# Selection masks, candidate pairs and expert tiles in the routing of a gMLP, attention and PEER block

## The chip, the cores and the metric

One core of a Trainium2 chip runs the whole program. The metric is the device time of one execution in microseconds (us). The engines are TensorE (PE, with its weight loads as PEld), VectorE (DVE), ScalarE (ACT), GpSimd (POOL) and the DMA queues that SyncE (SP), ACT and POOL issue. Each engine runs its own instructions in order; semaphores tie the engines together.

## The reference

For 512 tokens of width 1024 the block adds a mixing branch and then an expert branch. What the change touches is the expert branch (PEER): eight heads each score 2 x 128 sub keys, keep the best 16 of either half, form the sums of pairs, keep the best 16 pairs, and so choose 16 of 16,384 experts.

```python
q = (xb @ w_query).reshape(PEER_TOKEN_BLOCK, PEER_HEADS, 2, PEER_HALF)
sc = jnp.einsum('thpd,hpkd->thpk', q, sub_keys).astype(jnp.float32)
s_top, i_top = lax.top_k(sc, PEER_TOPK)
cand = s_top[:, :, 0, :, None] + s_top[:, :, 1, None, :]
cand_idx = i_top[:, :, 0, :, None] * PEER_NKEYS + i_top[:, :, 1, None, :]
...
best, pos = lax.top_k(cand, PEER_TOPK)
eidx = jnp.take_along_axis(cand_idx, pos, axis=-1)
g = jax.nn.softmax(best, axis=-1)
u = jnp.take(expert_u, eidx, axis=0)
h = jax.nn.gelu(jnp.einsum('thkd,td->thk', u, xb))
vv = jnp.take(expert_v, eidx, axis=0)
return jnp.einsum('thk,thkd->td', (g * h.astype(jnp.float32)).astype(xb.dtype), vv)
```

## The kernel before

The 512 tokens are four tiles of 128. The program runs in four stages: mixing (to about 240 us), routing (to about 455 us), gates (to about 622 us) and the loop over expert chunks (to the end).

**Dense and gathered tokens.** Three token tiles (ND = 3), less their last 64 tokens, do the expert branch densely: 128 expert tiles, each a load of 512 KB (`raw`), a split into `hi` (ACT, line 124) and `lo` (line 125, on DVE or POOL), and 24 matmuls of 320 columns (three products for each of 8 depth steps, lines 140 to 142) into one of two PSUM buffers `pu`, which ACT empties with a GELU into `act` (line 546). Sums of such tiles are later multiplied with gates and with the rows of `expert_v`. The remaining 64 tokens have their rows of `expert_u` gathered: 64 "early rows" of 128 x 1024, each an indirect DMA on POOL (line 480) and a dot product on DVE (line 489, one operand `xbu` in PSUM). The first token tile is gathered wholly in the last stage.

**Routing.** Iteration h of the loop in lines 665 to 684 issues up to EARLY = 7 early rows into ROWA = 8 row buffers, then `candidates(h)`: two projections of 24 matmuls of 512 columns each into PSUM tiles `pa` (four buffers), one expert tile before the key scores and one after (FILL = 1, counted in chunks of two tiles), eight small key-score products (line 649), and the top 16 of six score tiles on DVE (`top16`, 30 instructions). Then `pairs` and `choose` of the head before: `pairs` copies positions to floats on ACT (lines 580, 581) and adds pairs on DVE, seven `tensor_tensor` instructions with both operands in SBUF (line 588). `choose` spreads the pair indices into `tree` (line 595, a copy on POOL), takes the top 16 of the pair sums, makes six bit masks of the positions in one `tensor_tensor` of the positions and a constant `bits` (line 601, both in SBUF, result in a PSUM tile `pa`), and selects with them in six predicated copies (line 613). The result `eidx` (line 615) feeds the row indices of the next early rows (line 495). After head 7 an iteration without a head makes BRIDGE = 8 expert tiles, the softmax over all heads follows (line 621), and routing ends. By then 26 expert tiles are begun (2 + 16 + 8).

**Gates.** Lines 779 to 831 are written out in order for PE, DVE, ACT and POOL. `indices_of` turns `eidx` into two index rows (lines 703 to 706), `gates_of` transposes them on PE (lines 712 to 714). Then 48 steps, each of 8 tokens: DVE makes two one-hot arrays `bm` and `am` (lines 728, 738), POOL multiplies `bm` by the gates (line 730), ACT makes a part of `am` (lines 742, 744), PE multiplies them (line 751, 16 instructions a step) and ACT copies the result out (line 754); every two steps 1 MB is stored. Beside that a step issues one early row while there are any, and multiplies a few depth steps of an expert tile so that 40 tiles are done after the last step (`made`, `left`, `some`); six more follow.

**Order.** In routing a scheduler orders each engine's instructions by priority and its own estimates. In the gate stage the order is the code's. In the loop PE's order is the code's. A PSUM or SBUF tile of a pool with n buffers waits until the tile n allocations earlier has been read for the last time: the mask tile of head h takes a `pa` buffer that the second key-score tile of head h + 2 takes after it.

```python
nc.vector.tensor_tensor(mask.rearrange("p (l n) -> p l n", l=6),
                        bpos.rearrange("p t k -> p (t k)")[:, None, :]
                        .to_broadcast([P, 6, n * TOPK]),
                        bits[:, :, None].to_broadcast([P, 6, n * TOPK]), op=ALU.bitwise_and)
```

## Time and profile before

| what | value |
| --- | --- |
| median of three runs | 1493.92 us (1490.16 to 1494.91) |
| the profiled execution's own time | 1489.67 us |
| its span, first to last instruction | 1487.9 us |
| mean granted TensorE clock | 0.984 of full speed |
| PE busy, share of the span | 94% |
| DVE | 78% |
| ACT | 43% |
| POOL | 46% |

Shares of the whole span hide the stages, so the rows below go stage by stage: first the busy time of each engine in each stretch, then single instructions. Idle time in a row stands in brackets with what ended it. In the table of stretches a PE that is busy for the whole stretch is the bound there; a PE with idle time while DVE is busy for the whole stretch is not.

### The profile page before, as it was taken

What the parts mean: (1) busy time and instruction counts of PE and PEld (TensorE: products, weight loads), DVE (VectorE), ACT (ScalarE), POOL (GpSimd) and SP (SyncE); (2) the same over time, 40 slices, a digit from 0 to 9 for tenths busy, and PEclk for the clock granted to TensorE, in tenths of its full rate; (3) what the DMA queues carried; (4) which work ended last, traced back from release to release, by engine and by line L of the source; (5) the groups of instructions that cost most, each with busy time, mean ns of one, the idle gap of its engine ahead of it and who ended that gap; (6) DMA issues with size and microseconds to landing.
All of it is one profiled execution on the core that took longest, in us unless ns stands there. A gap on an engine that the chain in (4) does not pass through costs nothing.

```text
span 1487.9 us, 21702 instructions
## 1 busy us (share of the span) xinstructions
PE 1403.9 (94%) x7804; PEld 1235.9 (83%) x7804; DVE 1158.7 (78%) x2345; ACT 641.9 (43%) x1108; POOL 690.4 (46%) x470
## 2 busy tenths in 40 slices
PE   7999999998878888999989899999999999999998
PEld 6886678987777888888978799888999989888886
DVE  5437554699996968688988789898888888688883
ACT  5447534332335677743434333343343333333331
POOL 0000016687867966504435555464555554344530
PEclk9999999998998999999999999999999999999999
DMA  5352226576765976878878799999999999879992
GB/s 184 114 184 71 86 102 186 184 260 230 282 230 165 324 219 198 240 256 310 300 284 331 290 376 330 350 355 349 389 350 357 368 341 367 305 285 341 333 356 85
DMA packets 161420, 396.78 MB, mean 267 GB/s; under 512 B 12304, under 2 KB 74528, under 8 KB 159264
## 3 DMA queue, kind: packets, MB, share of 16 engines
q1 hardware_dynamic: 62992, 197.42, 37.4%
q0 software_dynamic: 47488, 171.50, 31.1%
q10 hardware_dynamic: 50832, 26.48, 6.3%
q8 instruction: 61, 1.00, 0.3%
q14 instruction: 47, 0.39, 0.1%
HBM read 363.86 MB, written 31.46 MB: 266 GB/s over the span
## 4 chain that ended last, share of the span: by engine, by line
PE 51%; DVE 19%; DMA 13%; issue 7%; POOL 5%; ACT 4%; ACTq 0%; SPq 0%; DVEq 0%; POOLq 0%
PE pu L140 6%; PE pu L142 6%; PE pu L141 6%; PE pa L932 5%; PE pa L933 5%; PE pa L936 5%; DMA row<-in_vd,eint 5%; DVE rowe L489 3%; PE px L933 3%; PE px L932 3%; PE px L936 3%; DMA row<-in_ud,eint 3%; PE pa L140 2%; PE pa L141 2%; PE pa L142 2%
## 5 line engine op out<-in xcount | busy, mean ns | idle before, releaser
L124 ACT ACTIVATE hi<-raw 128x1024 fp32r<-128x1024 f32 x300 | 317.3, 1058 | 511.0 <-DMA raw<-in_vd 185.2
L125 DVE TENSOR_TENSOR lo<-raw,hi 128x1024 fp32r<-128x1024 f32 x251 | 309.5, 1234 | 109.5 <-ACT hi L124 108.4
L874 POOL DMA_INDIRECT row<-in_vd,eint x128 | 196.9, 1538 | 196.8 <-DVE acc L876 165.2
L863 POOL DMA_INDIRECT row<-in_ud,eint x128 | 184.6, 1442 | 190.3 <-DVE row L865 149.1
L140 PE MATMUL pu<-xch,hi 128*128 128x320 f32 x816 | 257.7, 316 | 3.5 <-ACT act L546 2.9
L142 PE MATMUL pu<-xch,lo 128*128 128x320 f32 x816 | 252.6, 310 | 2.6 <-POOL lo L125 2.0
L141 PE MATMUL pu<-xcl,hi 128*128 128x320 f32 x816 | 252.5, 309 | 0.0
L932 PE MATMUL pa<-hi,wh 128*128 128x512 f32 x512 | 200.9, 392 | 0.0
L933 PE MATMUL pa<-lo,wh 128*128 128x512 f32 x512 | 200.5, 392 | 0.0
L876 DVE SCALAR_TENSOR_TENSOR acc<-row,hw,acc 128x1024 f32<-128x1024 f32 x128 | 165.1, 1290 | 40.4 <-DMA row<-in_vd,eint 40.1
L865 DVE SCALAR_TENSOR_TENSOR row<-row,xb 128x1024 f32<-128x1024 f32 x128 | 156.3, 1223 | 28.9 <-DMA row<-in_ud,eint 28.5
L140 PEld LDWEIGHTS pu<-xch,hi 128*128 128x128 f32 x816 | 154.7, 190 | 7.2 <-ACT act L546 5.0
L936 PE MATMUL pa<-hi,wl 128*128 128x512 f32 x512 | 158.1, 390 | 0.0
L142 PEld LDWEIGHTS pu<-xch,lo 128*128 128x128 f32 x816 | 154.3, 189 | 3.8 <-POOL lo L125 2.2
L141 PEld LDWEIGHTS pu<-xcl,hi 128*128 128x128 f32 x816 | 154.6, 189 | 1.5
L125 POOL TENSOR_TENSOR lo<-raw,hi 128x1024 fp32r<-128x1024 f32 x49 | 117.8, 2416 | 77.2 <-ACT hi L124 73.3
L751 PE MATMUL pa<-bm,am 128*128 128x128 f32 x768 | 99.0, 283 | 19.9 <-POOL bm L730 13.7
L751 PEld LDWEIGHTS pa<-bm,am 128*128 128x128 f32 x768 | 93.3, 196 | 25.1 <-POOL bm L730 22.6
L932 PEld LDWEIGHTS pa<-hi,wh 128*128 128x128 f32 x512 | 96.8, 189 | 20.6
L933 PEld LDWEIGHTS pa<-lo,wh 128*128 128x128 f32 x512 | 96.8, 189 | 20.5
L936 PEld LDWEIGHTS pa<-hi,wl 128*128 128x128 f32 x512 | 96.6, 189 | 20.6
L933 PE MATMUL px<-lo,wh 128*128 128x512 f32 x256 | 101.0, 395 | 7.2 <-DVE lo L125 7.2
(215 smaller groups left out, 2635.1 us busy)
## 6 DMA issues: line engine op xcount, KB each, us to landing
raw<-in_uT SPq DMA_DIRECT2D x128, 512.0 KB, 5.8
raw<-in_vd SPq DMA_DIRECT2D x128, 512.0 KB, 5.6
gd<-gst ACTq DMA_DIRECT2D x24, 1024.0 KB, 6.2
gc<-gd SPq DMA_DIRECT2D x15, 1536.0 KB, 9.7
raw<-in_w_in SPq DMA_DIRECT2D x20, 512.0 KB, 4.7
raw<-in_wq SPq DMA_DIRECT2D x16, 512.0 KB, 3.8
raw<-in_w_out SPq DMA_DIRECT2D x8, 512.0 KB, 4.2
bt<-in_bias SPq DMA_DIRECT2D x8, 256.0 KB, 7.4
```

The costliest lines, as they stand in the source:

```text
L124: nc.scalar.activation(hi, raw, AF.Copy)
L125: eng.tensor_tensor(lo, raw, hi.bitcast(F32), op=ALU.subtract)
L140: nc.tensor.matmul(ps, lh[0], rh[0], start=first, stop=False)
L141: nc.tensor.matmul(ps, lh[0], rh[1], start=False, stop=False)
L142: nc.tensor.matmul(ps, lh[1], rh[0], start=False, stop=last)
L751: nc.tensor.matmul(ps[:, i * P:(i + 1) * P], am[:, 4 * q + i, :], bm[:, 4 * q + i, :], start=True, stop=True)
L863: nc.gpsimd.indirect_dma_start(out=row, out_offset=None, in_=ud, in_offset=bass.IndirectOffsetOnAxis(ap=eint[:, j:j + 1], axis=0))
L874: nc.gpsimd.indirect_dma_start(out=row, out_offset=None, in_=vd, in_offset=bass.IndirectOffsetOnAxis(ap=eint[:, j:j + 1], axis=0))
L876: nc.vector.scalar_tensor_tensor(acc0, row, hw[:, j:j + 1], acc0, op0=ALU.mult, op1=ALU.add)
L932: nc.tensor.matmul(accs[t][half], wh[:, b, tok], w[b][0][:, ds_], start=first, stop=False)
L933: nc.tensor.matmul(accs[t][half], wh[:, b, tok], w[b][1][:, ds_], start=False, stop=False)
L936: nc.tensor.matmul(accs[t][half], wl[:, b, tok], w[b][0][:, ds_], start=False, stop=last)
```

## The change

In routing, six `tensor_scalar` instructions, one for each bit, take the place of the one mask instruction and its constant `bits`. `pairs` gets a part of the mask's PSUM tile, into which ACT copies the best scores and the scaled positions of the first half; the seven additions read them there and their other operand in SBUF. The tree copy goes from POOL to ACT. Six early rows instead of seven are issued for each head, into six buffers instead of eight. FILL becomes a list in tiles: two for heads 0 to 3, three for heads 4 to 7, so that 30 tiles are begun in routing instead of 26; `act` slots are taken when a tile is opened. `pairs` of the last head and the softmax are not scheduled before the fourth and the sixth of the eight bridging tiles has been activated. `indices_of` of the first gate tile and the split of two more expert tiles go ahead of the softmax's end, and the gate stage begins with one whole expert tile before and another after its first transposes. In the gate stage the last tile's `gates_of` is made two steps earlier. In the last stage `choose` uses the six instructions too, with masks in SBUF and the tree copy on POOL as before.

```diff
-ROWA = 8
+ROWA = 6
-EARLY = 7
+EARLY = 6
-SOME = 14
-FILL = 1
+SOME = 15
+FILL = (2, 2, 2, 2, 3, 3, 3, 3)
...
-        def pairs(pool, top, pos, n):
-
-            nc.scalar.activation(top[:, 1, :, 0, :], pos[:, :, 0, :], AF.Copy, scale=float(NK))
+        def pairs(pool, top, pos, n, ps=None):
+
+            if ps is None:
+                first = top[:, :, :, 0, :]
+            else:
+                first = ps.rearrange("p (a t r) -> p a t r", a=2, r=TOPK)
+                nc.scalar.copy(first[:, 0], top[:, 0, :, 0, :])
+            nc.scalar.activation(first[:, 1], pos[:, :, 0, :], AF.Copy, scale=float(NK))
...
-                                        a[:, :, 0, i:j, None].to_broadcast(full), op=ALU.add)
+                                        f[:, :, i:j, None].to_broadcast(full), op=ALU.add)
...
-            nc.gpsimd.tensor_copy(tree, cand[:, 1, :, None, 0:32].to_broadcast([P, n, TOPK, 32]))
+            spread(tree, cand[:, 1, :, None, 0:32].to_broadcast([P, n, TOPK, 32]))
...
-            nc.vector.tensor_tensor(mask.rearrange("p (l n) -> p l n", l=6),
-                                    bpos.rearrange("p t k -> p (t k)")[:, None, :]
-                                    .to_broadcast([P, 6, n * TOPK]),
-                                    bits[:, :, None].to_broadcast([P, 6, n * TOPK]), op=ALU.bitwise_and)
+            for i in range(6):
+                nc.vector.tensor_scalar(mask[:, i * n * TOPK:(i + 1) * n * TOPK], bpos.rearrange("p t k -> p (t k)"),
+                                        1 << i, None, op0=ALU.bitwise_and)
...
-                for _ in first_products(len(acts) * BC, BRIDGE, nc.gpsimd, True):
-                    pass
+                for i, _ in enumerate(first_products(sum(FILL) + BC, BRIDGE, nc.gpsimd, True)):
+                    behind.append(done[0])
...
-                mask = pa()[:, 0:6 * ND * TOPK].bitcast(U32)
+                ps = pa()
+                mask = ps[:, 0:6 * ND * TOPK].bitcast(U32)
...
-                choose(rq, pairs(rq, *cands.pop(0), ND), ND, gate[:, GT:, hs], eidx[:, GT:, hs], mask, tree)
+                with tc.issue_after(behind[BRIDGE // 2 - 1]) if behind else ExitStack():
+                    cand = pairs(rq, *cands.pop(0), ND, ps[:, 6 * ND * TOPK:8 * ND * TOPK])
+                choose(rq, cand, ND, gate[:, GT:, hs], eidx[:, GT:, hs], mask, tree, nc.scalar.copy)
...
-        softmax(rq, gate[:, GT:, :].rearrange("p t (h k) -> p (t h) k", k=TOPK), ND * NH)
+        ff = {0: indices_of(GT)}
...
+        for _ in range(HELD):
+            split_next()
+        with tc.issue_after(behind[-3]):
+            softmax(rq, gate[:, GT:, :].rearrange("p t (h k) -> p (t h) k", k=TOPK), ND * NH)
...
-            ff[0] = indices_of(GT)
-            split_next()
+            multiply_tile()
             gs[0] = gates_of(GT, ff.pop(0))
             split_next()
+            multiply_tile()
```

On DVE in routing, head 0, this stood from the mask on before (`pa` is the mask, `top`, `pos` and `scr` belong to the keys of a later head):

```order
L601 TENSOR_TENSOR pa<-bpos,bits 128x288
L613 COPY_PREDICATED tree<-pa,cand 128x48x18
L563 MAX top<-scr 128x8 x2
L564 MAX_INDEX pos<-top,scr 128x8
L565 MATCH_REPLACE rep<-top,scr 128x128
```

And this stands there now:

```order
L607 TENSOR_SCALAR pa<-bpos 128x48 x6
L617 COPY_PREDICATED tree<-pa,cand 128x48x18
L617 COPY_PREDICATED tree<-pa,tree 128x48x16
L617 COPY_PREDICATED tree<-pa,tree 128x48x8
L617 COPY_PREDICATED tree<-pa,tree 128x48x4
L617 COPY_PREDICATED tree<-pa,tree 128x48x2
L617 COPY_PREDICATED tree<-pa,tree 128x48
L619 COPY eidx<-tree 128x3x16
L562 MAX top<-scr 128x8 x2
```

The selections of a head stand together now, and all 30 key instructions of the next head stand ahead of its pairs; in heads with early rows the dot products lie between the six mask instructions, and the first few key instructions of the next but one head lie between the selections.

On ACT in the middle of routing, from the store of key scores to the next head's projection, this stood before:

```order
L656 DMA s0d<-s_2375 128x256
L124 ACTIVATE hi<-raw 128x1024
L546 ACTIVATE act<-pu 128x320
L580 ACTIVATE top<-pos 128x3x16
L581 CAST top<-pos 128x3x16
L641 COPY qt<-pa 128x512
L124 ACTIVATE hi<-raw 128x1024 x2
```

And now:

```order
L584 ACTIVATE pa<-pos 128x48
L660 DMA s0d<-s_2368 128x256
L124 ACTIVATE hi<-raw 128x1024
L547 ACTIVATE act<-pu 128x320
L585 CAST top<-pos 128x3x16
L600 COPY tree<-cand 128x1536
L645 COPY qt<-pa 128x512
L124 ACTIVATE hi<-raw 128x1024 x2
```

The tree copy stands in front of the copy of the next projection, so that copy and the splits behind it wait for DVE's pairs.

On PE at the end of routing, the transposes of the first gates stood behind the last routing tile (`pu<-xbh`), and the first tile of the gate stage (`pu<-xch`) behind them:

```order
L141 MATMUL pu<-xbl,hi 128x320
L142 MATMUL pu<-xbh,lo 128x320
L712 MATMUL pa<-ident,ff 128x128
L713 MATMUL pa<-ident,ff 128x128
L714 MATMUL pa<-ident,gate 128x128
L140 MATMUL pu<-xch,hi 128x320
```

Now they stand behind the 24 matmuls of a gate-stage tile:

```order
L141 MATMUL pu<-xcl,hi 128x320
L142 MATMUL pu<-xch,lo 128x320
L731 MATMUL pa<-ident,ff 128x128
L732 MATMUL pa<-ident,ff 128x128
L733 MATMUL pa<-ident,gate 128x128
L140 MATMUL pu<-xch,hi 128x320
```

Between the transposes and the first product of one-hots PE has 18 matmuls of a tile before and 36 (a tile and a half) now. In the 48 steps it has three or two depth steps beside the products before, and two or one now; from the first product of the loop's chunks on, PE's order is the same.

## Rows read from the trace of the kernel before

**Rows 1.** Busy time of each engine in seven stretches of the span: us, then each engine's busy us (number of instructions), the granted clock, the DMA share and GB/s.

```profile
248.90:327.80 78.90, 78.90 (x450) 71.31 (x449) 64.38 (x332) 28.09 (x54) 56.16 (x39) 1.00 0.64 217
327.80:408.00 80.20, 66.09 (x340) 58.66 (x339) 80.20 (x340) 23.89 (x44) 61.12 (x49) 0.91 0.71 254
408.00:462.80 54.80, 42.22 (x253) 40.42 (x251) 50.08 (x137) 19.38 (x37) 33.76 (x24) 0.91 0.50 170
462.80:515.80 53.00, 46.62 (x341) 45.36 (x342) 44.61 (x53) 35.65 (x81) 49.50 (x32) 0.94 0.94 302
515.80:621.80 106.00, 92.61 (x734) 88.93 (x733) 79.36 (x81) 81.50 (x189) 73.86 (x39) 1.00 0.74 216
621.80:855.00 233.20, 219.14 (x1193) 196.35 (x1194) 196.20 (x476) 93.64 (x138) 91.88 (x64) 0.98 0.81 294
855.00:1302.00 447.00, 446.45 (x2452) 402.57 (x2451) 379.98 (x483) 169.08 (x240) 231.99 (x159) 1.00 0.95 353
```

**Rows 2.** Timeline of PE, the key-score products of heads 0, 3, 5 and 7 (start in us, duration in us).

```profile
248.93 1.95 PE L649 MATMUL pa<-skt,qt 128*128 128x128 f32 x16
308.11 1.95 PE L649 MATMUL pa<-skt,qt 128*128 128x128 f32 x16
353.35 1.95 PE L649 MATMUL pa<-skt,qt 128*128 128x128 f32 x16
408.03 1.95 PE L649 MATMUL pa<-skt,qt 128*128 128x128 f32 x16
```

**Rows 3.** Timeline of PE: two matmuls of expert tiles at full clock, 59 matmuls apart; then the two waits of the bridging tiles (idle time and what ended it in brackets), the first transpose of the gates, and the first product of one-hots.

```profile
431.02 0.31 PE L140 MATMUL pu<-xbh,hi 128*128 128x320 f32 x1
...
439.68 0.31 PE L142 MATMUL pu<-xbh,lo 128*128 128x320 f32 x1
...
427.67 0.64 PE L140 MATMUL pu<-xbh,hi 128*128 128x320 f32 x1 [3.66 <-ACT act L546]
428.10 0.47 PE L141 MATMUL pu<-xbl,hi 128*128 128x320 f32 x1
428.37 0.47 PE L142 MATMUL pu<-xbh,lo 128*128 128x320 f32 x1
...
444.71 0.64 PE L140 MATMUL pu<-xbh,hi 128*128 128x320 f32 x1 [4.72 <-ACT act L546]
...
455.18 0.33 PE L712 MATMUL pa<-ident,ff 128*128 128x128 f32 x1 [1.67 <-ACT ff L706]
...
462.85 2.05 PE L751 MATMUL pa<-bm,am 128*128 128x128 f32 x16 [0.22 <-POOL bm L730]
```

**Rows 4.** Line 601 as a whole (duration in ns: least, median, most), its two long instances in DVE's timeline, and what POOL ran meanwhile.

```profile
L601 DVE TENSOR_TENSOR pa<-bpos,bits x8: 442/464/7272, 262.2 to 442.3; 128x288 uint32<-128x288 uint32 x8
...
343.60 6.77 DVE L601 TENSOR_TENSOR pa<-bpos,bits 128x288 uint32<-128x288 uint32 x1
...
418.20 7.27 DVE L601 TENSOR_TENSOR pa<-bpos,bits 128x288 uint32<-128x288 uint32 x1
...
342.94 7.10 POOL L125 TENSOR_TENSOR lo<-raw,hi 128x1024 fp32r<-128x1024 f32 x3
...
418.06 7.08 POOL L125 TENSOR_TENSOR lo<-raw,hi 128x1024 fp32r<-128x1024 f32 x3
```

**Rows 5.** Lines 588 and 704 as a whole, as in the group before.

```profile
L588 DVE TENSOR_TENSOR cand<-top x84: 166/186/1087, 258.5 to 787.8; 128x48 f32<-128x48 f32 x16, 128x24 f32<-128x24 f32 x12, 128x96 f32<-128x96 f32 x8, 128x30 f32<-128x30 f32 x8
...
L704 DVE TENSOR_SCALAR ii<-ei x3: 227/1608/2383, 454.3 to 556.8; 128x128 int32<-128x128 int32 x3
```

**Rows 6.** Groups of instructions in 245 to 450 us, shapes kept apart: busy us, mean ns of one, then the idle time of the engine before them.

```profile
L125 POOL TENSOR_TENSOR lo<-raw,hi 128x1024 fp32r<-128x1024 f32 x35 | 83.5, 2402 | 22.1 <-ACT hi L124 21.8
...
L489 DVE SCALAR_TENSOR_TENSOR rowe<-rowe,px 128x1024 f32<-128x1024 f32 x48 | 58.5, 1223 | 5.1 <-DMA rowe<-in_ud,eui 5.1
L480 POOL DMA_INDIRECT rowe<-in_ud,eui x49 | 46.9, 958 | 17.8 <-issue 11.1 <-DVE rowe L489 4.1 <-PE pu L142 0.6
...
L595 POOL COPY tree<-cand 128x1536 f32<-128x1536 f32 x8 | 12.0, 1496 | 0.9 <-DVE cand L588 0.6
...
L588 DVE TENSOR_TENSOR cand<-top 128x18 f32<-128x18 f32 x8 | 1.4, 171 | 0.0
```

**Rows 7.** Groups of instructions in 450 to 640 us, shapes kept apart, columns as in rows 6.

```profile
L730 POOL TENSOR_TENSOR bm<-bm,gt 128x1024 f32<-128x1024 f32 x48 | 90.8, 1899 | 22.5 <-DVE bm L728 21.1
L728 DVE TENSOR_TENSOR bm<-iota_k,pa 128x1024 f32<-128x1024 f32 x48 | 58.4, 1216 | 10.7 <-PE pa L751 8.3 <-ACT ni L719 1.8 <-POOL lo L125 0.6
...
L738 DVE TENSOR_TENSOR am<-iota_k,pa 128x768 f32<-128x768 f32 x48 | 45.5, 947 | 0.0
...
L489 DVE SCALAR_TENSOR_TENSOR rowe<-rowe,px 128x1024 f32<-128x1024 f32 x17 | 20.6, 1220 | 3.6 <-DMA rowe<-in_ud,eui 3.6
```

**Rows 8.** Timeline of DVE: two results of routing, of heads 3 and 5.

```profile
359.57 0.23 DVE L615 COPY eidx<-tree 128x48 f32<-128x48 f32 x1
...
404.08 0.24 DVE L615 COPY eidx<-tree 128x48 f32<-128x48 f32 x1
```

**Rows 9.** DVE at the end of routing: timeline of the first addition of head 7's pairs and of its result, then the group of early rows between them (432.2 to 451.6 us; columns as in rows 6).

```profile
432.12 0.67 DVE L588 TENSOR_TENSOR cand<-top 128x96 f32<-128x96 f32 x1
...
451.41 0.23 DVE L615 COPY eidx<-tree 128x48 f32<-128x48 f32 x1
...
L489 DVE SCALAR_TENSOR_TENSOR rowe<-rowe,px 128x1024 f32<-128x1024 f32 x7 | 8.6, 1226 | 0.0
```

**Rows 10.** Timeline of PE: products of one-hots at steps 2, 14 and 47 of 0 to 47, and at three steps in the middle (21 to 23).

```profile
473.13 1.95 PE L751 MATMUL pa<-bm,am 128*128 128x128 f32 x16
...
515.80 2.02 PE L751 MATMUL pa<-bm,am 128*128 128x128 f32 x16
...
621.78 2.05 PE L751 MATMUL pa<-bm,am 128*128 128x128 f32 x16 [1.14 <-POOL bm L730]
...
539.79 1.95 PE L751 MATMUL pa<-bm,am 128*128 128x128 f32 x16
542.46 1.95 PE L751 MATMUL pa<-bm,am 128*128 128x128 f32 x16
546.42 2.05 PE L751 MATMUL pa<-bm,am 128*128 128x128 f32 x16 [1.14 <-DVE bm L728]
```

More of the change, by code (lines that the diff above doesn't have):

```diff
@@ L511, in weights_early @@
                                         dots[own].rearrange("p a b k -> p (a b k)"), op=ALU.mult)
-        ready, begun, more = [], [], []
+        ready, begun, more, done, behind = [], [], [], [], []
         def split_tile(i, eng):
-            c, b = divmod(i, BC)
-            if b == 0:
-                slot = c % (AHEAD + 1)
-                acts[c] = (actp if slot < SOME else more[0]).tile([P, BC, NDU], F32, name="act", tag=f"act{slot}")
-            ready.append((c, b, load_split(uT[i], eng, b=P)))
+            ready.append((*divmod(i, BC), load_split(uT[i], eng, b=P)))
         open_tile = []
@@ L530, in multiply_some @@
                     open_tile.extend((*ready.pop(0), pu(), 0))
+                    if open_tile[1] == 0:
+                        c = open_tile[0]
+                        slot = c % (AHEAD + 1)
+                        acts[c] = (actp if slot < SOME else more[0]).tile([P, BC, NDU], F32, name="act",
+                                                                          tag=f"act{slot}")
                 c, b, (hi, lo), ps, k0 = open_tile
@@ L554, in first_products @@
                 yield
-        bits = rt.tile([P, 6], U32, name="bits")
-        for i in range(6):
-            nc.vector.memset(bits[:, i:i + 1], 1 << i)
         s0d = dram.tile([NH, P, 2 * NK], F32, name="s0d")
@@ L583, in pairs @@
             a = top.rearrange("p a t q r -> p (a t) q r")
+            f = first.rearrange("p a t r -> p (a t) r")
             c = cand.rearrange("p a t n -> p (a t) n")
@@ L659, in candidates, with indices_of @@
             return top, pos
+        def indices_of(t):
+            ei = gat.tile([P, NH * TOPK], I32, name="ei", tag="ei", bufs=1)
+            ii = gat.tile([P, 2, NH * TOPK], I32, name="ii", tag="ii", bufs=1)
+            ff = gat.tile([P, 2, NH * TOPK], F32, name="ff", tag="ff", bufs=2)
+            nc.scalar.copy(ei, eidx[:, t, :])
+            nc.vector.tensor_scalar(ii[:, 0, :], ei, 7, None, op0=ALU.logical_shift_right)
+            nc.vector.tensor_scalar(ii[:, 1, :], ei, NK - 1, None, op0=ALU.bitwise_and)
+            nc.scalar.copy(ff, ii)
+            return ff
         for _ in first_products(0, BC, nc.vector, True):
@@ L812, in hybrid_block @@
                     weights_early(1)
+                if n == own - 3:
+                    late = gates_of(GT + t, ff.pop(t))
                 if n == own - 1:
-                    gs[t] = gates_of(GT + t, ff.pop(t))
+                    gs[t] = late
                 made = len(ready) * KT + (KT - open_tile[4] if open_tile else 0)
```

31 lines of the change are left out of this document (11 added, 20 removed).

## The prediction

> **What bounds the kernel now.** I read the busy times stage by stage first [rows 1]. From 248.9 to 327.8 us PE is busy for the whole stretch: routing's first heads are bound by PE. From 327.8 to 408.0 us DVE is busy for the whole stretch (80.20 of 80.20) and PE for 66.09: the later heads, which carry early rows, are bound by DVE, and the granted clock falls to 0.91. From there to the first product of one-hots (462.85 us) PE works 42.22 of 54.80 us, again at 0.91. The gate stage has two halves: while early rows run, the DMA share is 0.94; afterwards no engine is full. From 855 us on PE is busy 446.45 of 447.00 us, and the change leaves its order there as it was. So what can be won lies between 248.9 and 621.8 us.
>
> PE's pace in routing is read from the key-score products [rows 2]: heads 0 to 3 follow each other every 59.18 / 3 = 19.7 us, heads 5 to 7 every 54.68 / 2 = 27.3 us. An expert tile costs PE 24 matmuls; 59 of them took 8.66 us [rows 3], so 0.147 us each and 3.52 us a tile. With no wait and full clock, the kernel before would have reached its first product of one-hots at 248.9 + 7 x 19.7 (all heads have two tiles) + 1.95 (last key scores) + 9 x 3.52 (rest of head 7 and bridge) + 3 (transposes, 18 matmuls) = 423 us. It came at 462.85. The 39 us are 14.1 + 12.6 us of idle PE [rows 1] and about 12 us of matmuls at a lower clock: after a wait they are 0.27 us apart instead of 0.147 [rows 3].
>
> **The masks and pairs.** Six of the eight mask instructions took about 0.46 us; two took 6.77 and 7.27 us [rows 4]. Both started within 0.7 us of a run of three `lo` subtractions on POOL and ended with it. That is 6.3 + 6.8 = 13.1 us of DVE in the stretch that DVE bounds. The seven additions of the pairs show the same in small (median 0.19 us, longest 1.09 [rows 5]); perhaps 2 us over all heads. The six new mask instructions are smaller than anything of this kind in the trace; the nearest row is the smallest addition, 0.17 us [rows 6], and with overlap they may take half of that, so 0.5 to 1.0 us for 0.46. I take +0.3 us a head.
>
> The Trainium skill, page "SBUF — State Buffer", section "Who interferes with whom", says that a VectorE instruction with two SBUF inputs contends with a GpSimd instruction that reads SBUF, that the later one waits until the earlier has ended, and that one with at most one SBUF input outside the two-port modes does not contend; the trace agrees, 6.77 us behind a 7.10 us run. The same section names `tensor_scalar`, the new mask, among those that can enter a two-port mode, which speaks against the change. "VectorE: DVE Perf Modes", section "Why PSUM operands drop a tier", excludes these modes for any PSUM operand, and routing's masks are written to PSUM; by the two pages nothing of the 13.1 us comes back.
>
> **Early rows, tree copy.** One row less for each of seven heads takes 7 x 1.22 = 8.5 us from DVE in routing [rows 6] and puts them into the gate stage, where the same instruction takes 1.22 us [rows 7]. A head in the DVE-bound stretch with no long mask takes (404.08 - 359.57) / 2 = 22.3 us [rows 8]; it becomes 22.3 - 1.2 + 0.3 = 21.4. The tree copy leaves POOL (1.5 us [rows 6]) for ACT, which is busy 23.9 of 80.2 us [rows 1]: no cost as work. Its place in front of the projection's copy makes ACT wait for DVE's pairs; that counts among the waits below.
>
> **Expert tiles.** Heads 4 to 7 get a third tile, 4 x 3.52 = 14.1 us of PE moved out of the gate stage. From head 4 on PE then needs 19.7 + 3.5 = 23.2 us a head, more than DVE's 21.4, so PE becomes the bound. Each tile also brings a 512 KB load, a `hi` on ACT and a `lo` of 2.40 us on POOL; POOL gives up 1.5 (tree) and 0.96 (a gather) [rows 6], so its 61.1 / 3 = 20.4 us a head [rows 1] stay as they are.
>
> **The end of routing.** Now PE waits 3.66 and 4.72 us for `act` [rows 3], which stands on ACT behind the softmax and the last pairs; the change puts these behind the fourth and sixth bridging tile, and a whole tile ahead of the transposes. The chain behind the fourth tile runs on DVE from head 7's pairs to its result, 19.5 us before, of which 8.6 were early rows that do not stand there now [rows 9]; 3.5 us more led to the first transpose [rows 3, 9]: 14.4 us. PE has four bridging tiles and one gate-stage tile then, 17.6 us. I take the cover as sufficient; without it PE would wait 2 to 5 us.
>
> **Sum to the first gates.** Key scores of head 7 at 248.9 + 4 x 19.7 + 3 x 23.2 = 397.4; + 1.95 + 10 x 3.52 + 3.52 + 0.4 (transposes) = 438.5. From there to the first product it took 7.7 us before [rows 3]; the least is one-hot and gate product, 1.2 + 1.9 = 3.1 us [rows 7]. I take 5, since only one `lo` instead of two stands ahead on POOL: 443.5. Then the waits that remain: heads 2 and 3 have two tiles and early rows, so DVE's 21.4 stands against 19.7 (3.4 us); the mask's buffer is the one that the second key-score product of the head after next needs, and the selections now end only as that head's keys begin (3 us for the heads where PE arrives first); 2 us at the tail. Together 8 us, with 0 and 20 (half of today's 39) as ends. First product at 451.5 instead of 462.85: **-11.3 us** (ends -19 and +1).
>
> **The gate stage.** Before, the 47 intervals from 462.85 to 621.78 us are 2 of 5.1, 12 of (515.80 - 473.13) / 12 = 3.56 with early rows, and 33 of 3.21 [rows 3, 10]. Afterwards 22 rows remain instead of 15, so about 20 intervals keep 3.56: DVE's 1.22 + 0.95 + 1.22 + part of a `lo` make 3.5 [rows 7], and the DMA share leaves no room. The other 25 lose one of two depth steps: a plain step takes 2.67, one with a new tile 3.96 [rows 10], now every eighth step instead of every fourth. PE could go at 2.67 - 3 x 0.147 = 2.23, POOL at 1.90. I take 2.75 with the new tiles. 2 x 4 + 20 x 3.56 + 25 x 2.75 = 148 us instead of 159: **-11 us**. Ends: 2.5 a step gives -17, 3.21 as now gives 0.
>
> **The rest.** Six tiles, the loop and the output stay: 0. The masks of the last stage grow by 0.3 to 0.7 us four times on DVE, beside a PE that is full from 855 us on and nearly full before [rows 1]: 0, at most 3.
>
> Sum: -22 us on 1489.67 is 1467.4. The profiled execution is 4.25 us below the median of 1493.92; by the median **1472 us**.
>
> **Rivals.** *All is hidden*: no waits in routing and 145 us of gates, 19 + 14 us less, 1461. For it: PE did run four heads without a wait. Against: DVE and PE lie within 2 us of each other in six heads.
>
> *The waits come back elsewhere*: PE, DVE and POOL all near 20 to 23 us a head, and each hands over to the next, so 16 us of waits remain and the gates take 153: 3 + 6 us less, 1485. For it: POOL is 20.4 us busy of 23.2, the mask's buffer ties PE to DVE more closely.
>
> *The mask waits on as a `tensor_scalar`*: line 704, a `tensor_scalar`, takes 0.23 to 2.38 us [rows 5], so this kind can wait too. Two of 6.5 us among eight again: 10 of the 13 us would come through, 1482. Against: line 704 lies in SBUF on both sides, the new masks do not. This is also the case in which the change does not do what it says.
>
> *Six row buffers stop POOL, slower*: eight gathers stand in a row on POOL now with six buffers, so the seventh waits for a dot product of the same head, and four `lo` of 2.40 us stand behind it. POOL has 23.2 - 20.3 = 3 us of slack a head. A wait of 3 us costs nothing; one of 8.5 us costs 5.5 us in each of heads 3 to 7, 27 us: 1499. Slower begins at about 8.3 us. For it: today, with eight buffers, gathers already wait for a row once (4.1 us [rows 6]). Against: it was one time of 49.
>
> **How the numbers follow.** Forecast 58%, its own range 1464 to 1481; all hidden 11%; waits elsewhere 18%; mask waits 5%; POOL stops 8%. The bound for faster or slower is 0.3% (4.5 us), about what a measurement of this kernel can tell from no change: below 1489.4 or above 1498.4. Faster: 58 + 11 + 5 + 10 of the 18 = 84%; within: 8%; slower: 8%. Range 1460 to 1488: it leaves out the slow case, half of the waits elsewhere and a little below.
>
> **What the changed profile would show.** No mask above 0.3 us; key scores of heads 4 to 7 some 23 us apart, head 7's at 398 to 410; no wait for `act` above 2 us in the bridge and the granted clock near 1.0 up to the gates; first product of one-hots at 445 to 458; early steps of 3.5 us, late ones of 2.5 to 2.9; the same 866 us after the last product. It is wrong if key scores are over 25 us apart (POOL's gathers or the mask's buffer will be named as what ended the wait), or if late gate steps stay at 3.2.

## The result and the profile after

In the first comparison the changed kernel took 1486.03 us (median of 7 runs, 1481.24 to 1489.43) and the kernel before 1495.02 us (7 runs, 1490.16 to 1500.46): ratio 0.9938, 95% interval 0.9915 to 0.9962, 9 us less. On two other chips the changed kernel took 1485.79 and 1485.94 us, the kernel before 1505.2 and 1502.09 us: ratios 0.9875 (0.9853 to 0.9897) and 0.9899 (0.9870 to 0.9927). So the change makes the kernel faster by 0.6 to 1.3%; the forecast was 1472 us, 14 us lower than what came.

The profiled execution took 1489.41 us, only 0.26 us less than that of the kernel before (1489.67). It is among the longest of its runs, and that of before was shorter than all seven runs that its median stands for. The stretches of the changed kernel, columns as in [rows 1] (first three: heads 0 to 3, heads 4 to 6, head 7 and bridge):

```profile
249.90:328.80 78.90, 78.90 (x450) 71.31 (x450) 58.31 (x328) 33.85 (x61) 50.06 (x33) 1.00 0.57 193
328.80:407.40 78.60, 72.44 (x411) 65.34 (x410) 70.96 (x322) 29.96 (x54) 59.61 (x45) 0.98 0.76 267
407.40:464.60 57.20, 50.93 (x320) 49.70 (x319) 45.64 (x180) 24.46 (x44) 35.56 (x24) 0.91 0.53 168
464.60:618.60 154.00, 126.80 (x938) 119.65 (x939) 130.50 (x149) 109.86 (x261) 120.87 (x74) 0.94 0.84 260
618.60:855.00 236.40, 223.67 (x1211) 200.34 (x1210) 201.29 (x501) 94.13 (x140) 92.92 (x64) 0.97 0.82 295
855.00:1302.00 447.00, 444.46 (x2443) 400.62 (x2442) 375.45 (x479) 170.40 (x242) 231.74 (x158) 1.00 0.95 351
```

Heads 0 to 3 are as before. In heads 4 to 6 VectorE's work fell from 80.20 us to 70.96, but the stretch is only 1.6 us shorter: now PE is 92% busy there, with more work (72.44 us instead of 66.09). Behind head 7 VectorE works 45.64 us instead of 50.08 in a stretch that is 2.4 us longer. The timeline of PE gives the marks of [rows 2, 3, 10] (key scores of heads 4 and 7, first transpose, first and last product of one-hots), and below it stand the masks and the pairs as in [rows 4, 5]:

```profile
328.79 1.95 PE L653 MATMUL pa<-skt,qt 128*128 128x128 f32 x16
...
407.37 1.95 PE L653 MATMUL pa<-skt,qt 128*128 128x128 f32 x16
...
458.23 0.27 PE L731 MATMUL pa<-ident,ff 128*128 128x128 f32 x1
...
464.63 2.05 PE L770 MATMUL pa<-bm,am 128*128 128x128 f32 x16
...
618.64 1.95 PE L770 MATMUL pa<-bm,am 128*128 128x128 f32 x16
```

```profile
L607 DVE TENSOR_SCALAR pa<-bpos x48: 193/207/211, 282.2 to 449.9; 128x48 uint32<-128x48 uint32 x48
...
L593 DVE TENSOR_TENSOR cand<-top,pa x56: 167/183/263, 278.1 to 443.2; 128x48 f32<-128x48 f32 x16, 128x96 f32<-128x96 f32 x8, 128x30 f32<-128x30 f32 x8, 128x24 f32<-128x24 f32 x8
```

No mask takes over 0.211 us and no pair over 0.263 us: every long one of before is gone. Still the first product comes at 464.6 us, 1.8 us later than before and 13.1 later than forecast; the gates take 154.0 us (before 158.9, forecast 148), the rest 868.9 (before 866.1). 13.1 + 6.0 + 2.8 = 21.9 us is the whole distance between the 1467.4 us forecast for a profiled execution and the 1489.41 measured.

### The profile page after: what moved, and what is told of

Its sections match the earlier page's. It is cut to its first block, busy times and chain, and to the rows that moved or that the text cites. A ratio compares the mean times of both kernels' runs of the same rounds, so it can differ in the third digit from the quotient of the medians.

```text
span 1487.5 us, 21777 instructions
## 1 busy us (share of the span) xinstructions
PE 1410.3 (95%) x7804; PEld 1238.6 (83%) x7804; DVE 1143.3 (77%) x2397; ACT 651.7 (44%) x1124; POOL 682.8 (46%) x464
## 4 chain that ended last, share of the span: by engine, by line
PE 48%; DMA 17%; DVE 11%; issue 10%; POOL 8%; ACT 4%; ACTq 0%; SPq 0%; DVEq 0%; POOLq 0%
PE pu L140 7%; PE pu L142 7%; PE pu L141 7%; DMA row<-in_vd,eint 4%; PE pa L945 4%; PE pa L946 4%; PE pa L949 4%; DMA row<-in_ud,eint 3%; DMA raw<-in_uT 3%; DVE lo L125 3%; POOL lo L125 3%; DMA gc<-gd 3%; PE pa L140 2%; PE pa L142 2%; PE pa L141 2%
## 5 line engine op out<-in xcount | busy, mean ns | idle before, releaser
L125 DVE TENSOR_TENSOR lo<-raw,hi 128x1024 fp32r<-128x1024 f32 x249 | 305.0, 1226 | 107.9 <-ACT hi L124 106.8
L140 PE MATMUL pu<-xch,hi 128*128 128x320 f32 x784 | 248.2, 317 | 2.4 <-ACT act L547 2.3
L142 PE MATMUL pu<-xch,lo 128*128 128x320 f32 x784 | 242.8, 310 | 0.8 <-DVE lo L125 0.6
L141 PE MATMUL pu<-xcl,hi 128*128 128x320 f32 x784 | 242.9, 310 | 0.0
L125 POOL TENSOR_TENSOR lo<-raw,hi 128x1024 fp32r<-128x1024 f32 x51 | 123.5, 2435 | 81.5 <-ACT hi L124 76.8
L140 PEld LDWEIGHTS pu<-xch,hi 128*128 128x128 f32 x784 | 148.8, 190 | 5.9 <-ACT act L547 4.4
L142 PEld LDWEIGHTS pu<-xch,lo 128*128 128x128 f32 x784 | 148.5, 189 | 1.9 <-DVE lo L125 1.3
L141 PEld LDWEIGHTS pu<-xcl,hi 128*128 128x128 f32 x784 | 148.8, 190 | 1.4
L770 PE MATMUL pa<-bm,am 128*128 128x128 f32 x768 | 105.1, 291 | 27.3 <-POOL bm L749 12.7
L770 PEld LDWEIGHTS pa<-bm,am 128*128 128x128 f32 x768 | 97.6, 203 | 34.7 <-POOL bm L749 26.0
```

The costliest lines, as they stand in the source:

```text
L125: eng.tensor_tensor(lo, raw, hi.bitcast(F32), op=ALU.subtract)
L140: nc.tensor.matmul(ps, lh[0], rh[0], start=first, stop=False)
L141: nc.tensor.matmul(ps, lh[0], rh[1], start=False, stop=False)
L142: nc.tensor.matmul(ps, lh[1], rh[0], start=False, stop=last)
L770: nc.tensor.matmul(ps[:, i * P:(i + 1) * P], am[:, 4 * q + i, :], bm[:, 4 * q + i, :], start=True, stop=True)
```

## The experiments

Two questions: which part brings the gain, and what ate the rest of the forecast. Theory M: only masks and pairs together bring it, since whichever instruction still has two operands in SBUF meets POOL's runs. Theory S: the new order brings it. For the lost part, theory A: rows that land late and ACT's queue hold the later heads; theory B: the third tiles do. Names that begin with e_before and e_both are edits of the kernel before, the others of the changed one. Time is the median; "routing" runs from the first key score to the first product of one-hots in the profile; DVE is VectorE's busy time in it, the sum over its three stretches. The columns from DVE on are those of one profiled execution each, which need not be typical of the runs: those of e_early7 (1501.80 us) and e_pairs_sbuf (1506.95) were the longest of 12, that of e_after2 (1479.31) was the shortest of 6.

| run | time, us | before there | ratio (95%) | DVE, us | routing, us | first product | gates |
| --- | --- | --- | --- | --- | --- | --- | --- |
| (before, first profile) | | | | 194.7 | 213.9 | 462.8 | 158.9 |
| e_before | 1501.99 | 1503.05 | 0.9994 (0.9971 to 1.0017) | 203.1 | 225.4 | 475.5 | 159.2 |
| e_before_masks | 1504.19 | 1503.05 | 1.0011 (0.9994 to 1.0027) | 197.3 | 223.7 | 472.7 | 158.3 |
| e_before_both | 1490.28 | 1498.71 | 0.9944 (0.9923 to 0.9966) | 181.7 | 208.9 | 460.8 | 159.7 |
| e_both2 (the same) | 1490.18 | 1502.09 | 0.9907 (0.9877 to 0.9938) | 181.8 | 209.0 | 460.6 | 160.0 |
| (changed, first profile) | 1486.03 | 1495.02 | 0.9938 (0.9915 to 0.9962) | 174.9 | 214.7 | 464.6 | 154.0 |
| e_after | 1485.79 | 1505.2 | 0.9875 (0.9853 to 0.9897) | 172.3 | 213.2 | 463.2 | 154.2 |
| e_after2 | 1485.94 | 1502.09 | 0.9899 (0.9870 to 0.9927) | 174.7 | 211.4 | 460.4 | 152.9 |
| e_mask_one | 1491.62 | 1505.2 | 0.9904 (0.9872 to 0.9937) | 171.6 | 214.6 | 466.5 | 152.7 |
| e_pairs_sbuf | 1500.21 | 1498.71 | 1.0012 (0.9988 to 1.0037) | 186.1 | 224.0 | 476.0 | 153.8 |
| e_old_both | 1497.63 | 1498.71 | 1.0009 (0.9985 to 1.0032) | 182.5 | 223.8 | 475.9 | 153.6 |
| e_fill2 | 1483.69 | 1505.2 | 0.9865 (0.9840 to 0.9891) | 170.1 | 201.9 | 450.9 | 161.3 |
| e_fill2_rowa7 | 1487.32 | 1503.05 | 0.9889 (0.9859 to 0.9919) | 170.1 | 204.5 | 455.5 | 160.7 |
| e_rowa7 | 1483.42 | 1503.05 | 0.9879 (0.9848 to 0.9910) | 172.4 | 209.9 | 462.3 | 154.1 |
| e_early7 | 1489.19 | 1498.71 | 0.9942 (0.9918 to 0.9965) | 181.5 | 219.6 | 470.6 | 153.5 |
| e_tree_pool | 1492.41 | 1505.2 | 0.9912 (0.9884 to 0.9939) | 172.6 | 216.0 | 463.7 | 153.6 |
| e_no_hold | 1483.90 | 1502.09 | 0.9873 (0.9844 to 0.9903) | 171.1 | 210.4 | 461.1 | 153.8 |

### The kernel before, profiled again

No edit.

> The kernel before, profiled a second time. Its time and that of its own reference runs should agree within 3 us (ratio 1.000). What is to be read is the stage in which this profile is longer than the first one of it: if its runs spread by where the two long masks fall (theory C), the first one-hot product comes at 462 to 470 with a DVE mask of over 2 us in more or fewer heads, and the gates take 159 as before; if they spread by the expert loops behind the gates (theory D), the first product stays within 1 us of 462.8 and the stretch behind the gates is over 868.

The second profile has a span of 1500.5 us, 12.6 more than the first, and all of it lies ahead of the gates: first product at 475.5 instead of 462.8 (11.5 us of that in routing), gates 159.2, rest 865.8 (theory C; D falls). Its eight masks as a whole, the earliest long one in VectorE's timeline, POOL beside it, then ACT and PE behind it:

```profile
L601 DVE TENSOR_TENSOR pa<-bpos,bits x8: 452/1752/7559, 263.3 to 454.5; 128x288 uint32<-128x288 uint32 x8
...
294.20 7.56 DVE L601 TENSOR_TENSOR pa<-bpos,bits 128x288 uint32<-128x288 uint32 x1
...
294.32 7.10 POOL L125 TENSOR_TENSOR lo<-raw,hi 128x1024 fp32r<-128x1024 f32 x3
...
305.75 0.24 ACT L580 ACTIVATE top<-pos 128x48 f32<-128x48 uint32 x1 [8.45 <-DVE pos L567]
...
311.87 0.57 ACT L641 COPY qt<-pa 128x512 f32<-128x512 f32 x1
...
312.49 1.16 PE L649 MATMUL pa<-skt,qt 128*128 128x128 f32 x8 [3.11 <-ACT qt L641]
```

Here four masks are long (7.56, 6.41, 2.82 and 6.44 us), not two [rows 4]. The first of them makes VectorE late with the positions, ACT waits 8.45 us for these with the copy of the next projection behind it, and PE waits 3.11 us for that copy: the chain from a long mask to a late key score, in a head that had none in the first profile. The same kernel meets POOL's runs more or less often by execution.

### The masks alone, then masks and pairs, in the old order

```diff
-            nc.vector.tensor_tensor(mask.rearrange("p (l n) -> p l n", l=6),
...
+            for i in range(6):
+                nc.vector.tensor_scalar(mask[:, i * n * TOPK:(i + 1) * n * TOPK], bpos.rearrange("p t k -> p (t k)"),
```

> Of the whole change only the six-instruction mask, in the order of the kernel before. Each theory expects that no mask instruction takes over 0.3 us. The prediction's account (the long masks, 6.77 and 7.27 us, stand on the chain of the last heads): the key scores of head 7 come 4 to 7 us earlier than at 407.4, the first product at 452 to 458, and the time is 6 to 11 us below the kernel before. Theory E (one of the two lies ahead of head 7 beside other waits of PE and the other behind PE's own queue, so that other waits take their place): first product at 460 to 463, time within 3 us of the kernel before, and the gain of the whole change comes from elsewhere.

It gained nothing (theory E's time; its first product at 460 to 463 did not come). No mask is long, but the pairs are now: four of 2.23 to 5.66 us, where the second profile of before has none over 1 us. One in VectorE's timeline and POOL beside it:

```profile
358.98 4.36 DVE L588 TENSOR_TENSOR cand<-top 128x96 f32<-128x96 f32 x1
...
356.13 7.08 POOL L125 TENSOR_TENSOR lo<-raw,hi 128x1024 fp32r<-128x1024 f32 x3
```

The groups of masks and pairs in routing, before (second profile) and with the masks alone (busy us, mean ns):

```profile
L601 DVE TENSOR_TENSOR pa<-bpos,bits 128x288 uint32<-128x288 uint32 x8 | 25.3, 3163 | 0.7 <-DVE top L566 0.5
...
L588 DVE TENSOR_TENSOR cand<-top 128x48 f32<-128x48 f32 (+5 forms) x56 | 10.1, 239 | 0.3 <-ACT top L581 0.3
```

```profile
L588 DVE TENSOR_TENSOR cand<-top 128x48 f32<-128x48 f32 (+5 forms) x56 | 25.0, 491 | 0.3 <-ACT top L581 0.3
...
L602 DVE TENSOR_SCALAR pa<-bpos 128x48 uint32<-128x48 uint32 x48 | 9.9, 206 | 0.7 <-DVE top L566 0.3
```

The pairs went from 10.1 to 25.0 us: they took over the waits. With both parts:

```diff
+                nc.scalar.copy(first[:, 0], top[:, 0, :, 0, :])
+            nc.scalar.activation(first[:, 1], pos[:, :, 0, :], AF.Copy, scale=float(NK))
...
-                                        a[:, :, 0, i:j, None].to_broadcast(full), op=ALU.add)
+                                        f[:, :, i:j, None].to_broadcast(full), op=ALU.add)
```

> The kernel before with two parts of the change and nothing else: the six-instruction masks, and pairs whose broadcast operand is copied to PSUM by ScalarE. Theory M (in the old order whichever instruction of these two still has both operands in SBUF meets GpSimd's runs and holds ScalarE's queue behind it; the masks alone only handed the stall to the pairs): no mask and no pair over 0.3 us, the first product at 457 to 466 where the second profile of before has 475.5 and the masks alone 472.7, time 1486 to 1493, that is 9 to 16 us below the kernel before. Theory S (the gain of the change is its order: two or three tiles a head, rows, the splits): first product at 470 to 475, time within 4 us of the kernel before.

> The kernel before with masks and pairs alone, on the chip of the two others of this call. Theory M: 8 to 12 us below the kernel before, within 4 us of the changed kernel. Theory N: 8 to 10 us below the kernel before, and 6 to 12 us above the changed kernel.

Pairs and masks are short now, and the two parts give 8.4 us on one chip and 11.9 on another, the second beside the changed kernel (e_after2, below), which was 4.2 us faster with overlapping intervals. Theory M holds; of theory N these 4 us are left, and the runs can't tell them from nothing. The stretches of routing (columns as above):

```profile
251.90:330.80 78.90, 78.90 (x450) 71.26 (x449) 58.38 (x328) 29.88 (x58) 52.08 (x36) 1.00 0.58 192
330.80:394.90 64.10, 60.20 (x339) 53.49 (x338) 63.46 (x293) 21.56 (x45) 54.14 (x41) 1.00 0.82 282
394.90:460.80 65.90, 43.15 (x255) 41.02 (x254) 59.86 (x227) 19.02 (x40) 44.39 (x36) 0.82 0.62 205
```

Heads 4 to 6 take 64.10 us where [rows 1] has 80.20, and the clock there rises from 0.91 to 1.00. But VectorE is busy for 63.46 of them and 59.86 of the next 65.90: it works nearly without a pause, and PE waits 12.71 us in one piece for the first transpose:

```profile
453.08 0.45 PE L718 MATMUL pa<-ident,ff 128*128 128x128 f32 x1 [12.71 <-ACT ff L712]
```

### The old masks and the old pairs in the new order

```diff
-                                        1 << i, None, op0=ALU.bitwise_and)
...
+                                    bits[:, :, None].to_broadcast([P, 6, n * TOPK]), op=ALU.bitwise_and)
```

> The changed kernel with the masks made in one instruction from two SBUF operands as before, everything else changed. If a long mask still lies on the path that sets the end, two or three masks of 5 to 7 us come back and the time is 6 to 13 us above the changed kernel. Theory A allows less, 3 to 8 us, since DVE idles 2 to 3 us a head there. If the masks were never on the path: 0 to 2 us.

```diff
-                    cand = pairs(rq, *cands.pop(0), ND, ps[:, 6 * ND * TOPK:8 * ND * TOPK])
+                    cand = pairs(rq, *cands.pop(0), ND)
```

> The changed kernel with the old pairs (both operands in SBUF) and the new masks. Theory M: pairs of 3 to 6 us in two or more heads, as with the masks alone in the old order, first product at 465 to 472, time 1488 to 1496. Theory S: one such pair at most, first product at 463 to 466, time within 3 us of the changed kernel's 1485.9.

Both edits together:

> The changed kernel with the old one-instruction mask and the old pairs (both operands in SBUF), all else as changed. Theory M: masks or pairs of over 2 us in three or more heads, 10 to 25 us of them in all, first product at 469 to 478, time 1493 to 1502. Theory S: in the new order few of them meet a run of GpSimd, first product at 463 to 468, time 1485 to 1491.

With the old pairs the whole gain is gone, with or without the new masks: the change's order alone is worth nothing that can be measured (1.0009). With the old mask alone most of it stays: one long mask in the profile (2.15 us), time 5.8 us above e_after, intervals of the ratios overlapping. So in this order it is mostly the pairs that meet POOL: seven of 1.19 to 3.05 us where theory M had fewer and longer ones, and the first product is 4 us behind its range, in a profile 6.7 us above the median of its runs; that of both edits, at its median, has the same routing (223.8 us). One of seven long ones (its line holds it, 2.59 us, and a short one of 0.17 us behind it), and what POOL ran:

```profile
355.11 2.69 DVE L593 TENSOR_TENSOR cand<-top 128x30 f32<-128x30 f32 x2
...
355.21 2.43 POOL L125 TENSOR_TENSOR lo<-raw,hi 128x1024 fp32r<-128x1024 f32 x1
```

### The changed kernel again, and two tiles in every head

No edit, on two other chips:

> The changed kernel again, for a second profile of it. Theory A (hand-overs: in the later heads the rows that land late, ACT's queue and the key scores make a loop of about 26 us a head, whatever the masks cost) and theory B (the third tile of heads 4 to 7 is what PE, ACT and POOL cannot take in) both expect the same time, 1481 to 1489 us, key scores of heads 5 to 7 25 to 29 us apart and the first product of one-hots at 458 to 468 us. If it comes at 452 or before, the first profile was an outlier and the prediction's first term was right.

> The changed kernel a third time, beside the two parts alone (masks and pairs in the old order) on one chip. Theory M (masks and pairs are the whole gain; tiles, rows and tail pay for themselves): within 4 us of that kernel. Theory N (the rest of the change is worth as much again): 6 to 12 us below it.

The three times agree within 0.3 us; it is the kernel before that differs, 1495 to 1505 us by the chip.

```diff
-FILL = (2, 2, 2, 2, 3, 3, 3, 3)
+FILL = (2, 2, 2, 2, 2, 2, 2, 2)
```

> The changed kernel with two tiles in every head, 26 tiles begun in routing as before. Theory A: key scores of heads 5 to 7 stay 24 to 26 us apart, so routing gets 0 to 6 us shorter, and the gate stage takes the four tiles back, 6 to 10 us: 0 to 8 us slower in all. Theory B: key scores return to 21 to 22 us apart, 12 to 15 us off routing, and the whole is 3 to 8 us faster.

The stretches, columns as above:

```profile
328.00:396.10 68.10, 61.10 (x338) 53.56 (x338) 64.38 (x309) 25.08 (x47) 49.30 (x39) 1.00 0.75 263
396.10:450.90 54.80, 47.24 (x296) 46.27 (x296) 47.79 (x197) 23.67 (x44) 36.90 (x27) 0.91 0.61 201
450.90:612.20 161.30, 136.56 (x1037) 129.03 (x1036) 132.59 (x151) 116.80 (x269) 125.86 (x76) 0.98 0.84 260
```

Without the four third tiles heads 4 to 6 take 68.1 us instead of 78.6, and the first product comes at 450.9 instead of 463.2 (e_after). The gates take 7.1 us longer for it (161.3 against 154.2). By the medians two microseconds remain for two tiles, less than these runs can tell from nothing. With seven row buffers (below) the same step from three tiles to two is smaller in routing, 462.3 to 455.5, and the medians go the other way by 3.9 us. Theory B has the direction right in routing; for the whole kernel no run shows that the third tiles pay or cost.

### Row buffers, early rows, tree copy, holds

```diff
-ROWA = 6
+ROWA = 7
```

> The changed kernel with seven early row buffers instead of six. Theory A (rows that land late hold VectorE in the heads 4 to 7): VectorE's wait for early rows in 300 to 465 falls from 13 us to under 6, the first product comes at 457 to 461, time 3 to 8 us below the changed kernel. Theory B (the third tiles are what PE and ScalarE can't take in): the wait for rows gets shorter or moves, key scores of heads 4 to 7 stay 25 to 29 us apart, first product 462 to 465, time within 2 us of the changed kernel.

The same edit with two tiles in every head:

> Two tiles in every head and seven early row buffers. With two tiles alone the first product came at 450.9 and the time was 1483.7. Theory A: rows hold the loop here too, so the first product comes at 445 to 449 and the time is 1477 to 1481. Theory B: with two tiles a head PE is the bound up to head 4 and close to it behind, the buffer changes nothing: first product 450 to 452, time 1482 to 1486.

VectorE's wait for early rows, 13.2 us in e_after and 9.3 in e_after2, fell to 6.9 with three tiles and from 5.5 to 4.0 with two; first products at 462.3 and 455.5, times within the intervals of their partners. Counted from the first key score, routing is 3.3 us shorter than in e_after with three tiles (1.5 shorter than in e_after2) and 2.6 us longer with two. So no run shows that rows that land late set the pace, and the 3 to 8 us that theory A expected did not come.

```diff
-EARLY = 6
+EARLY = 7
```

> The changed kernel with seven early rows a head instead of six (49 of them ahead of the gates, 15 left). The prediction's account (a row less is 0.9 us of VectorE in each head, and VectorE sets the pace of the heads 4 to 7): key scores of head 7 and the first product 3 to 6 us later, 466 to 470, gates 2 to 4 us shorter, time 0 to 4 us above the changed kernel. Rival (rows are taken as they come, as many per head either way, and what is left at the end fits under PE's tail): first product within 2 us of 464, gates 2 to 5 us shorter, time 0 to 5 us below the changed kernel.

VectorE's dot products in heads 4 to 6 and behind head 7, first of the changed kernel, then with seven rows:

```profile
L489 DVE SCALAR_TENSOR_TENSOR rowe<-rowe,px 128x1024 f32<-128x1024 f32 x24 | 29.2, 1218 | 7.4 <-DMA rowe<-in_ud,eui 7.3
...
L489 DVE SCALAR_TENSOR_TENSOR rowe<-rowe,px 128x1024 f32<-128x1024 f32 x10 | 12.1, 1212 | 4.2 <-DMA rowe<-in_ud,eui 4.2
```

```profile
L489 DVE SCALAR_TENSOR_TENSOR rowe<-rowe,px 128x1024 f32<-128x1024 f32 x24 | 29.2, 1218 | 5.0 <-DMA rowe<-in_ud,eui 4.9
...
L489 DVE SCALAR_TENSOR_TENSOR rowe<-rowe,px 128x1024 f32<-128x1024 f32 x17 | 20.7, 1218 | 5.5 <-DMA rowe<-in_ud,eui 5.4
```

24 in both: eight a head either way, since rows are taken as their indices come. The seven rows that EARLY = 6 leaves out are missing behind head 7, 17 - 10, and this profile has its first product 6 us later, at 470.6, the number of the prediction's account by another way than its own. But it is 12.6 us above the median of its runs, heads 4 to 6 were no slower in it (75.2 us), and the stretch behind the gates took 875.5 us, where the three profiles without the edit have 864 to 871; so the 6 us are not shown to be typical. Its gates were no shorter (153.5). The time, 3.2 us above e_after2, is of another chip, so what the rows are worth in all stays open.

```diff
-                choose(rq, cand, ND, gate[:, GT:, hs], eidx[:, GT:, hs], mask, tree, nc.scalar.copy)
+                choose(rq, cand, ND, gate[:, GT:, hs], eidx[:, GT:, hs], mask, tree)
```

> The changed kernel with the tree copy on POOL as before. Theory A says the copy in ACT's queue, which waits for the pairs, holds back the splits and key-score copies behind it: without it key scores come 1 to 2 us closer a head, 3 to 8 us faster in all, if POOL's 1.5 us a head do not eat it. Theory B sees no part for it: within 3 us.

```diff
-                with tc.issue_after(behind[BRIDGE // 2 - 1]) if behind else ExitStack():
+                with ExitStack():
...
-        with tc.issue_after(behind[-3]):
+        with ExitStack():
```

> The changed kernel without the two holds at the end of routing (the last pairs behind the fourth bridging tile, the softmax behind the sixth). The prediction's account (without the holds ScalarE's queue stands behind VectorE's last pairs and softmax, and PE waits for the GELUs of the bridging tiles): waits of PE for act of 3 to 9 us more behind head 7, first product at 467 to 473, time 2 to 8 us above the changed kernel. Rival (head 7's keys come too late for the holds to matter): first product within 2 us of 464, time within 2 us.

The first product stays within 4 us of e_after and e_after2 in both (463.7 and 461.1). The tree copy on ACT may be worth something (1492.41 against 1485.79, the ratios' intervals overlap), and PE's waits for `act` behind head 7 add up to 6.5 us without it too; the holds do nothing that can be measured, and PE's waits for `act` behind head 7 are 5.7 us without them and 5.8 to 6.9 with them (three profiles).

## Why the prediction was wrong

**The step that failed is the waits that remain.** In "Sum to the first gates" they are put at 8 us behind a first product of 443.5 us, 2 of them at the tail. They came to 21.1 us in the first profile (464.6), to 19.7 and 16.9 in the two others of the changed kernel (463.2 and 460.4), at or near the upper end of 20 that the sum names. In the first profile 1.0 us is a later start of the heads, 9.0 is the pace of heads 4 to 6, and 11.2 lies behind head 7's key scores. The 3.4 us for heads 2 and 3 did not come: heads 0 to 3 took 78.9 us, PE's pace. The second step is the gate stage, 6.0 us short of its -11; the rest was 2.8 us longer than forecast.

**Masks and pairs: mechanism right, priced one by one wrong.** It is the `lo` runs on POOL that VectorE's instructions with two SBUF operands wait for. The Trainium skill, page "SBUF — State Buffer", section "Who interferes with whom", says the same, and that an instruction with at most one SBUF input, outside the two-port modes, does not contend; all 48 masks and 56 pairs of the changed routing agree (0.211 and 0.263 us at most). Together the two parts took 13.0 us from VectorE's time in routing against the first profile of before (194.7 to 181.7), near the 13.1 + 2 less 2.4 (8 x 0.3) of the forecast, and 21.4 against the second (203.1). What failed is the price of each: "13.1 us" and "perhaps 2 us" took the durations of the trace as what each instruction costs with the other gone. Masks alone gave nothing (1.0011), and in the changed order the gain is gone when the pairs alone are old (1.0012). And VectorE's time did not come back in full: those 13.0 us made routing 5.0 us shorter than in the first profile (213.9 to 208.9).

**The profile of before was a lucky one.** The sum was made against an execution with two long masks that ended routing at 462.8 us; the other profile has four and ends it at 475.5. This lowered what the parts could win against that profile; what is won against the median of before is more (9 to 19 us by the chip) than the profiles of the first comparison show (0.3).

**The pace of heads 4 to 6.** The forecast had PE as their bound at 23.2 us a head. Measured are 78.6 / 3 = 26.2 us, of which PE worked 24.1 (25.0 us a head in e_after2, 26.3 in e_after). With two tiles it is 22.7, where 21.4 of VectorE stood in the forecast. The third tiles are not mainly what the forecast mis-sized: by its own terms they cost 3 x (23.2 - 21.4) + 3.5 = 8.9 us up to the first product, and measured are 12.3 (463.2 against 450.9) and, with seven row buffers, 6.8 (11.3 and 5.4 counted from the first key score). Without them the same sum gives 442.6 us, and the runs gave 450.9 and 455.5: the waits are there with two tiles as well, most of them behind head 7's key scores, where two tiles took 54.8 us in place of 42.6.

**"Early rows" failed in place.** "One row less for each of seven heads" does not happen: eight dot products a head stay, and the pace of the later heads gets nothing from it. The size was right in VectorE's work: seven products are missing at the tail (12.1 us of them instead of 20.7, 8.6 less where 8.5 was forecast). What that is worth in time is not shown.

**"The end of routing" failed.** "I take the cover as sufficient": PE still waited 1.96 us and 3.98 us for `act`. These two waits, and about 4.2 us by which 35 products of 320 columns came some 0.27 us apart instead of 0.147, are the 10 us by which the way from head 7's key scores to the first transpose (50.9 us) exceeds the forecast's 40.7. At 431.32 us ACT's tree copy stood ahead of the GELU and waited 7.18 us for VectorE's pairs:

```profile
414.80 0.42 PE L140 MATMUL pu<-xbh,hi 128*128 128x320 f32 x1 [1.96 <-ACT act L547]
...
417.21 0.47 PE L142 MATMUL pu<-xbh,lo 128*128 128x320 f32 x1
417.47 0.47 PE L140 MATMUL pu<-xbh,hi 128*128 128x320 f32 x1
...
431.32 0.64 PE L140 MATMUL pu<-xbh,hi 128*128 128x320 f32 x1 [3.98 <-ACT act L547]
...
429.44 1.49 ACT L600 COPY tree<-cand 128x1536 f32<-128x1536 f32 x1 [7.18 <-DVE cand L593]
430.84 0.43 ACT L547 ACTIVATE act<-pu 128x320 f32<-128x320 f32 x1
```

The copy is not the whole of it: with the copy on POOL (e_tree_pool) PE waited 4.49 and 2.05 us for `act` in this stretch. Before the wait at 414.80, head 7's keys had been late on their way from PE: ACT copied them only from 414.64 us on, after a `hi` that waited 6.77 us for its load, although PE had begun the key scores at 407.37:

```profile
413.36 1.06 ACT L124 ACTIVATE hi<-raw 128x1024 fp32r<-128x1024 f32 x1 [6.77 <-DMA raw<-in_uT]
414.32 0.42 ACT L547 ACTIVATE act<-pu 128x320 f32<-128x320 f32 x1
414.64 0.47 ACT L656 COPY scr<-pa 128x384 f32<-128x384 f32 x1
```

The granted clock of the stretch is 0.91 again, where the forecast had it near 1.0. The holds had been named as the cure; without them the time is the same. In the first profile of before no split behind head 7 waited for its load; in the three of the changed kernel these waits add up to 10 to 16 us. What sets the loads' landing was not tried.

**Gate stage: -4.9 us instead of -11.** Late plain steps do run at PE's 2.23 us, as worked out. But the first 20 intervals took 74.2 us (8 + 18 x 3.56 = 72.1 forecast) and the other 27 took 79.8 (75.9): seven of these took 3.75 to 5.72 us, where the forecast had 3.96 for one with a new tile. A plain step from 538.85 to 541.07 us, and the longest, from 555.70 to 561.42, in which PE waits for ACT's copy out and then for POOL (what held the other six is not shown):

```profile
538.85 1.95 PE L770 MATMUL pa<-bm,am 128*128 128x128 f32 x16
541.07 2.00 PE L770 MATMUL pa<-bm,am 128*128 128x128 f32 x16
...
555.70 1.05 PE L770 MATMUL pa<-bm,am 128*128 128x128 f32 x8
557.53 1.16 PE L770 MATMUL pa<-bm,am 128*128 128x128 f32 x8 [0.78 <-ACT gst L773]
561.42 0.82 PE L770 MATMUL pa<-bm,am 128*128 128x128 f32 x5 [2.29 <-POOL bm L749]
```

**The rest and the rivals.** The 868.9 us behind the gates lie within what profiles of the changed kernel spread over (864.1 to 870.5). Of the rivals, *the waits come back elsewhere* had the time (1485), in part by luck: it had routing 3 us shorter and the gates 6, and the profiles show routing's end 1.8 us later, the gates 4.9 shorter and a median that fell by more than the profiled time did. Its waits of 16 us are nearer to the 17 to 21 measured than the forecast's 8; that hand-overs between PE, DVE and POOL are their cause is not shown. *All is hidden* fell with PE's waits, *the mask waits on* with 0.211 us. *Six row buffers stop POOL* fell too: no gather waited over 0.3 us for a row to be read, and a seventh buffer left the time as it was.

Open: what holds three-tile heads at 25 to 26 us where PE works 24, and what makes `act` late behind head 7; and whether the kernel before meets POOL's runs more often on some chips, since its time differs by chip and only two executions of it were profiled.

## What to carry to other kernels

If several instructions can be held by the same blocker, the trace shows the wait only on the one that came first; change all of them together, and price the group, not each by its own duration. Before a sum is made against one profile, look whether its time is typical of the runs, and take a second profile where the stalls depend on how two engines happen to meet. Work that is moved from one stage to another can be paid for in the first what it saves in the second: here the third tiles cost 5 to 12 us ahead of the gates and saved some 7 in them. And the waits that remain deserve a term for each stretch: the forecast had 2 us for a tail that had 11.

## What the runs showed of the hardware

Over the six profiles with an old form in them (before twice, e_before_masks, e_mask_one, e_pairs_sbuf, e_old_both), 27 masks or pairs of routing took over 1 us. Each of them ended 0.04 to 0.34 us after a `lo` subtraction on POOL ended, and up to three such subtractions in a row were waited for, with no turn between them. In five of the 27 the record of VectorE's instruction begins 0.10 to 0.57 us before POOL's first (294.20 against 294.32, above), and still VectorE is the one that waits; POOL's subtractions kept their 2.4 us. The dot products of the early rows, with one operand in PSUM, ran beside the same subtractions at 1.19 to 1.32 us (148 of them; the others took 1.19 to 1.28).
